# The output projection of a hybrid decoder block in 128x512 instead of 128x256 products, with a fourth weight buffer

## The chip, the core and the metric

The kernel runs on one core of one Trainium2 chip. The metric is the device time of one execution in microseconds (us). The core has five engines that run their own instruction queues in order and meet through semaphores: TensorE (PE, matrix products; PEld is its loading of the stationary operand), VectorE (DVE), ScalarE (ACT), GpSimd (POOL) and SyncE (SP), which here issues all DMA transfers.

## What is computed

A decoder block over 2048 tokens of width 1024: a state-space branch and an attention branch that picks 256 keys per query, both projected, gated and added (`merged`), then the output projection with the residual, then a gated feed-forward network. Everything is float32. The change touches the third of these lines:

```python
merged = (jax.nn.sigmoid(g_ssm) * (y_ssm @ w_proj_ssm[l])
          + jax.nn.sigmoid(g_att) * (y_att @ w_proj_attn[l]))
x = x + merged @ w_out[l]                      # 2048x1024 @ 1024x1024
h2 = _rms(x, norm2_g[l])
x = x + (jax.nn.silu(h2 @ w_ffn_gate[l]) * (h2 @ w_ffn_up[l])) @ w_ffn_down[l]
```

## The kernel before

**Products.** Each float32 operand is held as two parts, hi and lo, in a reduced format. `mm3` (line 406) makes one product out of three matmul instructions: hi by hi, hi by lo, lo by hi. A matmul has a stationary operand of 128 columns and a moving operand of up to 512 columns, and every matmul instruction comes with its own weight load.

**Stages.** The dense half of the network (`block`, line 1695) runs over four token blocks of 512 tokens, called first to fourth block here. In each block come, in this order: the two branch projections (rows `f<-act,ww` of the trace, 192 matmuls of 128x512), whose gated sum is split into `mg`; the output projection (`f<-ww,mg`, 384 matmuls of 128x256); the second norm and the transposes of the normed rows `ha`, `hb`, `hh` into `h` (`f<-ident,ha` and so on); gate and up products (`f<-h,ww`); down products (`f<-wd,at`), added into `x1`.

**The output projection** (lines 1800 to 1827) is cut into four column groups of 256. In each group it makes two passes, tokens 0 to 255 and 256 to 511. A pass is 48 matmuls into one PSUM bank that holds two token tiles side by side; then DVE adds the bank into `x1` (`x<-f,x`). The two weight buffers of a group serve both passes and are dropped in the second. After the first pass of the last group the norm of token tiles 0 and 1 begins: `factor` (a square with row sum on ACT, then `ss` on DVE and `rr` on POOL) and `norm` (`ha`, `hb` on DVE).

**Weights** come through a ring (`Rings`, line 290), in the fixed order of `weights()` (line 1662). In the first block a buffer is made on the chip: a raw tile of 512 KB is loaded (two raw buffers), ACT, POOL or DVE makes the hi part, POOL or DVE the lo part, and the pair of 1 MB (`ww`, for the down weights `wd`) is also stored to DRAM (`wc`). In the other three blocks the pair is loaded from `wc`. The ring for `ww` has three buffers (line 1984); a buffer is filled again after `drop`, and loads are issued in the order of the list only.

**Order.** Every instruction is recorded by `Pace` (line 52), which keeps a clock for each engine from fixed costs. Three streams of work (state space, attention with its top-k search, dense) are merged by it: a stream goes on when its inputs are due and, for search work, as long as DVE's queue is less than `AHEAD` = 7 us ahead of PE, or `TIGHT` = 0.5 us while `tight` is set. `tight` is set after the first pass of the last column group and cleared when the first gate and up products are recorded. While the search runs, four more PSUM banks are lent to the dense stream (`lend`, `bank`), beside its own three. Dense work on block n waits until attention has finished that block's tiles.

## Time and profile before

| | us |
|---|---|
| median of 3 runs | 3380.91 |
| lowest and highest | 3377.41, 3381.88 |
| the profiled execution, its own time | 3383.72 |
| span of the trace | 3381.7 |
| mean granted TensorE clock | 0.972 |
| output projection, first to fourth block: start to end | 1056.3 to 1106.8, 1668.9 to 1717.2, 2304.1 to 2352.7, 2965.2 to 3011.4 |

In rows of the trace a group reads: engine, operation, output tile<-input tiles, shapes, count. A bracket such as [6.13 <-DVE ss] gives the idle time of that engine just before the row, and what ended it. The granted clock is a share of 2.4 GHz; a stretch at 0.5 is the lower level, 1.2 GHz.

### The profile page before, as it was taken

How to read it: one execution, taken by the hardware profiler on the slowest of the kernel's cores; microseconds unless marked ns; L12 is line 12 of the kernel's file. 1: busy time of each engine (PE TensorE's matmuls, PEld its weight loads, DVE VectorE, ACT ScalarE, POOL GpSimd, SP SyncE). 2: the span in 40 equal slices, each digit the busy share in tenths (PEclk: the TensorE clock that was granted, in tenths of full speed). 3: DMA queues.
4: the chain of work that ended last, by engine and by line, in shares of the span. 5: the costliest groups of instructions: out<-in, count | busy, mean ns of one | idle time of the engine just before them, and what ended most of it. 6: DMA issues, size and time to landing. Idle time of an engine off the chain costs nothing. (4 is left out here: it accounts for less than half of the span.)

```text
span 3381.7 us, 44230 instructions
## 1 busy us (share of the span) xinstructions
PE 3185.2 (94%) x16296; PEld 2693.5 (80%) x16296; DVE 2122.2 (63%) x4540; ACT 1278.5 (38%) x2213; POOL 621.0 (18%) x620
## 2 busy tenths in 40 slices
PE   7999989899978999998989999998999999899999
PEld 6989768678757888876788888878788888698887
DVE  6565785555687666699686775867776666322223
ACT  3231445444552444355412443666124444010000
POOL 4333766522232221134100000000000000000000
PEclk9999999999989999999999999999999999999999
DMA  5734333535458766756745324375472332755554
GB/s 185 230 114 115 114 111 106 166 92 149 123 186 293 276 210 217 248 174 239 297 155 230 143 94 168 132 263 215 177 262 99 125 131 94 275 195 201 200 200 161
DMA packets 315015, 605.66 MB, mean 179 GB/s; under 512 B 46352, under 2 KB 198704, under 8 KB 284080
## 3 DMA queue, kind: packets, MB, share of 16 engines
q1 hardware_dynamic: 314800, 602.85, 51.2%
q8 instruction: 128, 2.10, 0.2%
q14 instruction: 87, 0.71, 0.1%
HBM read 434.70 MB, written 166.89 MB: 178 GB/s over the span
## 5 line engine op out<-in xcount | busy, mean ns | idle before, releaser
L206 PE MATMUL f<-h,ww 128*128 128x512 f32 (+1 forms) x4416 | 1016.7, 384 | 1.2 <-DVE h L206 0.8
L206 PEld LDWEIGHTS f<-h,ww 128*128 128x128 f32 x4416 | 802.4, 191 | 156.4 <-DVE h L206 1.8
L206 PE MATMUL f<-wd,at 128*128 128x512 f32 x2112 | 523.5, 400 | 41.1 <-DVE wd L206 10.6
L206 PEld LDWEIGHTS f<-wd,at 128*128 128x128 f32 x2112 | 399.6, 192 | 132.6 <-DVE x L206 12.7
L206 PE MATMUL gps<-hT,gw 128*128 128x512 f32 x1536 | 384.7, 401 | 4.6 <-ACT gsg L206 3.2
L206 ACT ACTIVATE jka<-S,tr 128x1536 bf16<-128x1536 f32 (+5 forms) x217 | 305.6, 1408 | 190.5 <-DVE tr L206 115.6
L206 PEld LDWEIGHTS gps<-hT,gw 128*128 128x128 f32 x1536 | 287.0, 192 | 68.0 <-ACT gsg L206 5.2
L206 DVE TENSOR_TENSOR x<-f,x 128x512 f32<-128x512 f32 x352 | 236.5, 687 | 103.2 <-PE f L206 102.5
L206 PE MATMUL mm<-w,hT 128*128 128x512 f32 (+1 forms) x1152 | 282.3, 402 | 8.9 <-DVE hT L206 6.4
L206 DVE TENSOR_TENSOR tl<-pt,th 128x512 fp32r<-128x512 f32 (+1 forms) x288 | 184.1, 658 | 137.2 <-ACT th L206 136.4
L206 PEld LDWEIGHTS mm<-w,hT 128*128 128x128 f32 x1152 | 240.3, 238 | 36.0 <-DVE hT L206 8.0
L206 DVE SCALAR_TENSOR_TENSOR t<-t,f 128x512 f32<-128x512 f32 (+1 forms) x125 | 83.5, 668 | 278.8 <-PE f L206 238.1
L206 ACT CAST th<-pt 128x512 fp32r<-128x512 f32 (+1 forms) x288 | 155.9, 564 | 234.7 <-PE pt L206 230.5
L206 PE MATMUL f<-act,ww 128*128 128x512 f32 x768 | 189.3, 406 | 29.2 <-POOL ww L206 9.7
L206 PEld LDWEIGHTS f<-act,ww 128*128 128x128 f32 x768 | 148.9, 196 | 69.4 <-POOL ww L206 22.2
L206 PE MATMUL f<-ww,mg 128*128 128x256 f32 x1536 | 188.9, 285 | 10.1 <-ACT ww L206 4.6
L206 PEld LDWEIGHTS f<-ww,mg 128*128 128x128 f32 x1536 | 187.1, 194 | 12.4 <-ACT ww L206 5.0
L206 ACT ACTIVATE P<-P,m 128x1024 f32<-128x1024 f32 (+7 forms) x192 | 172.3, 900 | 53.5 <-DVE m L206 53.4
L206 POOL TENSOR_TENSOR g<-g,g 128x512 f32<-128x512 f32 x31 | 39.9, 1286 | 811.8 <-DVE g L206 798.1
L206 PE MATMUL lg<-kk,q 128*128 128x512 f32 (+1 forms) x640 | 184.1, 389 | 2.4 <-DMA kk<-kk 2.4
L206 ACT ACTIVATE t<-f 128x512 f32<-128x512 f32 (+1 forms) x92 | 53.1, 577 | 333.6 <-PE f L206 333.5
L206 ACT CAST at<-t 128x512 fp32r<-128x512 f32 (+1 forms) x92 | 55.3, 601 | 326.4 <-DVE t L206 326.4
(361 smaller groups left out, 4508.9 us busy)
## 6 DMA issues: line engine op xcount, KB each, us to landing
ww<-wc SPq DMA_DIRECT2D x180, 1024.0 KB, 4.9
wd<-wc SPq DMA_DIRECT2D x66, 1024.0 KB, 8.4
wc<-ww SPq DMA_DIRECT2D x60, 1024.0 KB, 7.8
raw<-in_w_in_dram SPq DMA_DIRECT2D x104, 256.0 KB, 3.3
wc<-wd SPq DMA_DIRECT2D x22, 1024.0 KB, 7.4
x<-in_x_dram SPq DMA_DIRECT2D x32, 512.0 KB, 5.1
gate<-gsg SPq DMA_DIRECT2D x64, 256.0 KB, 2.2
g<-gate SPq DMA_DIRECT2D x64, 256.0 KB, 5.3
```

The costliest lines, as they stand in the source:

```text
L206: return f(*args, **kw)
```

## The change

The output projection is now cut into two column halves of 512. In each half a pass takes two token tiles into two PSUM banks, one bank per tile, and goes through four weight buffers `q` of 256 rows by 512 columns each; each buffer serves tile t and then tile t + 1 before the next is asked for. All four buffers of a half are held until the second pass, which drops them one after the other. A block has 192 matmuls of 128x512 where it had 384 of 128x256, in four passes of 48 instead of eight, and still eight additions into `x1`, of 512 columns of one tile instead of 256 columns of two. The first bank of a pass is taken from the dense stream's own three, the second from either pool. The norm of tiles 0 and 1 and `tight` come after the first pass of the second half, so that 48 matmuls of 128x512 follow instead of 48 of 128x256. The loader is asked after every product (`tick`) instead of after every pair. The ring for `ww` has four buffers in all stages.

```diff
-        for cg in range(4):
-            for b in range(2):
-                items.append(("w", lambda raw, cg=cg, b=b: [
-                    (raw.rearrange("p (k c) -> p k c", k=4),
-                     a["w_out"][0, b * 512:(b + 1) * 512, cg * 256:(cg + 1) * 256]
+        for half in range(2):
+            for q in range(4):
+                items.append(("w", lambda raw, half=half, q=q: [
+                    (raw.rearrange("p (k c) -> p k c", k=2),
+                     a["w_out"][0, q * 256:(q + 1) * 256, half * 512:(half + 1) * 512]
                      .rearrange("(k p) c -> p k c", p=128))]))
...
-                for cg in range(D // NC):
-                    cl = slice(cg * NC, (cg + 1) * NC)
+                for half in range(2):
+                    cl = slice(half * 512, (half + 1) * 512)
                     for t in range(0, nt, 2):
-                        for k in range(KD):
-                            if k % 2 == 0:
-
-                                late = t == nt - 2 and k >= 4
-                                w = ld.get("w", 0 if late or k < 4 else 1)
-                                w = w.rearrange("p z a (k c) -> p (z a) k c", k=4)
-                                yield ready(w, mg) if k == 0 else at("PE", w)
-                            if k == 0:
-                                ps = bank()
+
+                        ps = []
+                        for q in range(4):
+                            w = ld.get("w", q if t < nt - 2 else 0)
+                            w = w.rearrange("p z a (k c) -> p (z a) k c", k=2)
                             for j in range(2):
+                                yield ready(w, mg) if q == 0 else at("PE", w)
+                                if q == 0:
+                                    ps.append(bank(j == 1))
                                 tl = slice((t + j) * 128, (t + j + 1) * 128)
-                                self.mm3(ps[:, j * NC:(j + 1) * NC], mg[:, 0, k, tl], mg[:, 1, k, tl],
-                                         w[:, 0, k % 4], w[:, 1, k % 4], k == 0 and j == 0, k == KD - 1 and j == 1)
-                            if t == nt - 2 and k % 4 == 3:
+                                for k in range(2):
+                                    g = q * 2 + k
+                                    self.mm3(ps[j], mg[:, 0, g, tl], mg[:, 1, g, tl], w[:, 0, k], w[:, 1, k],
+                                             g == 0, g == KD - 1)
+                                    ld.tick()
+                                if q == 3:
+
+                                    nc.vector.scalar_tensor_tensor(x1[:, t + j, cl], ps[j], 0.5, x1[:, t + j, cl],
+                                                                   op0=ALU.mult, op1=ALU.add)
+                            if t == nt - 2:
                                 ld.drop("w")
-                            ld.tick()
-
-                        nc.vector.scalar_tensor_tensor(x1[:, t:t + 2, cl], ps.rearrange("p (t c) -> p t c", t=2),
-                                                       0.5, x1[:, t:t + 2, cl], op0=ALU.mult, op1=ALU.add)
-                        if cg == D // NC - 1 and t == 0:
+                        if half == 1 and t == 0:
                             self.pace.tight = True
...
-                wp = self.pool(st, "fw", 3)
+                wp = self.pool(st, "fw", 4)
...
-                ld.ring("w", wp, 3)
+                ld.ring("w", wp, 4)
```

The order of the instructions shifts in all later stages, since `Pace` merges the streams anew. Three places are shown.

DVE, second block, before: the end of a round of the search (`jkd`, `uf`, `tf`), the addition of the last column group for tiles 0 and 1 (`x<-f,x`), and the norm of these tiles.

```order
L206 SCALAR_TENSOR_TENSOR jkd,cnt_13631<-H_13800,tf_13632,jkd 128x640
L206 TENSOR_SCALAR uf_13633<-cnt_13631 128x2
L206 SCALAR_TENSOR_TENSOR tf_13632<-uf_13633,tf_13632 128x2
L206 SCALAR_TENSOR_TENSOR x_14698<-f,x_14698 128x2x256
L206 TENSOR_SCALAR ss_15507<-ss_15507 128x1
L206 SCALAR_TENSOR_TENSOR ha<-x_14698,rr_15508,gB 128x1024
L206 TENSOR_SCALAR ss_15514<-ss_15514 128x1
L206 SCALAR_TENSOR_TENSOR hb<-x_14698,rr_15515,gB 128x1024
L206 SCALAR_TENSOR_TENSOR x_14698<-f,x_14698 128x2x256
```

The same place on DVE now:

```order
L206 SCALAR_TENSOR_TENSOR jkd,cnt_13395<-H_13529,tf_13396,jkd 128x640
L206 TENSOR_SCALAR uf_13397<-cnt_13395 128x2
L206 SCALAR_TENSOR_TENSOR tf_13396<-uf_13397,tf_13396 128x2
L206 SCALAR_TENSOR_TENSOR x_14508<-f,x_14508 128x512 x2
L206 TENSOR_SCALAR ss_15083<-ss_15083 128x1
L206 SCALAR_TENSOR_TENSOR ha<-x_14508,rr_15084,gB 128x1024
L206 TENSOR_SCALAR ss_15090<-ss_15090 128x1
L206 SCALAR_TENSOR_TENSOR hb<-x_14508,rr_15091,gB 128x1024
L206 SCALAR_TENSOR_TENSOR x_14508<-f,x_14508 128x512 x2
```

The norm still stands right behind the additions, with search work in front of them; between the two groups of additions PE now has a pass of 48 wide products instead of 48 narrow ones.

ACT, first block, before: the last parts of `mg`, the hi parts of weight buffers (`ww<-raw`; the first of these rows is the first buffer of the output projection) and the last steps of the search (`fin`).

```order
L206 CAST ww<-raw 128x1024
L206 CAST mg<-g_9735 128x512
L206 CAST ww<-raw 128x1024 x2
L206 ACTIVATE fin,ssum<-S_7045,nT 128x1024
L206 CAST ww<-raw 128x1024 x3
L206 ACTIVATE fin,ssum<-S_7204,nT 128x896
```

The same place on ACT now:

```order
L206 CAST ww<-raw 128x1024
L206 CAST mg<-g_9735 128x512
L206 CAST ww<-raw 128x1024 x3
L206 ACTIVATE fin,ssum<-S_7045,nT 128x1024
L206 CAST ww<-raw 128x1024 x2
L206 ACTIVATE fin,ssum<-S_7204,nT 128x896
```

Four buffers of the output projection, all that the first pass needs, now stand ahead of the first `fin`; three did.

PE, end of the third block and start of the fourth, before: the last value products of attention (`po<-tl,v`), its two closing products (`lg<-ident,s` turns the row sums, `lg<-r,hsel` spreads their reciprocals), down products, and the first projection of the fourth block (`f<-act,ww`).

```order
L206 MATMUL po<-tl,v 128x256
L206 MATMUL f<-h_20700,ww 128x512 x12
L206 MATMUL lg<-ident,s 8x128
L206 MATMUL f<-wd,at 128x512 x18
L206 MATMUL lg<-r_25857,hsel 128x128 x8
L206 MATMUL f<-wd,at 128x512 x78
L206 MATMUL f<-act_25848,ww 128x512 x24
```

The same place on PE now:

```order
L206 MATMUL po<-tl,v 128x256
L206 MATMUL f<-wd,at 128x512 x24
L206 MATMUL lg<-ident,s 8x128
L206 MATMUL lg<-r_25427,hsel 128x128 x8
L206 MATMUL f<-act_24977,ww 128x512 x24
```

The close of the last attention tile moved behind the down products of the third block: 96 of them stood between the turned sums and the fourth block, and none does now.

## Rows read from the trace of the kernel before

**Rows 1.** Page, engines: busy us (share of the span), instructions.

```profile
PE 3185.2 (94%) x16296; PEld 2693.5 (80%) x16296; DVE 2122.2 (63%) x4540; ACT 1278.5 (38%) x2213; POOL 621.0 (18%) x620
```

**Rows 2.** Groups of PE by line: names, shapes, count | busy, mean ns | idle before.

```profile
L206 PE MATMUL f<-wd,at 128*128 128x512 f32 x2112 | 523.5, 400 | 41.1 <-DVE wd L206 10.6 <-DVE x L206 9.5 <-DMA wd<-wc 7.2
...
L206 PE MATMUL f<-ww,mg 128*128 128x256 f32 x1536 | 188.9, 285 | 10.1 <-ACT ww L206 4.6 <-DMA ww<-wc 2.6 <-POOL ww L206 2.0
```

**Rows 3.** Stretches of the four output projections: engines, PEclk, DMA share, GB/s.

```profile
1056.30:1106.80 50.50, 48.49 (x384) 48.22 (x385) 38.40 (x74) 15.23 (x20) 11.06 (x7) 0.93 0.85 302
1668.90:1717.20 48.30, 46.77 (x385) 46.17 (x383) 43.33 (x125) 8.92 (x12) 1.29 (x1) 1.00 0.55 192
...
2965.20:3011.40 46.20, 46.20 (x387) 46.18 (x386) 8.61 (x14) 2.92 (x5) 2.38 (x3) 1.00 0.53 186
```

**Rows 4.** Timeline, fourth block: start us, us, engine, group [idle before <-releaser].

```profile
2965.22 46.23 PE L206 MATMUL f<-ww,mg 128*128 128x256 f32 x384
...
3045.59 0.60 ACT L206 ACTIVATE t<-f 128x512 f32<-128x512 f32 x1 [4.09 <-PE f L206]
...
3056.47 0.60 ACT L206 ACTIVATE t<-f 128x512 f32<-128x512 f32 x1 [4.09 <-PE f L206]
```

**Rows 5.** Who PE waited for: us in total, times, longest us.

```profile
PE f L206 <- DVE ss L206: 13.2, 2, 7.1
...
PE f L206 <- DMA act<-att: 3.6, 3, 1.4
...
PE f L206 <- DMA ww<-wc: 2.6, 3, 1.3
```

**Rows 6.** Timeline, second block, after the output projection.

```profile
1719.11 0.69 DVE L206 SCALAR_TENSOR_TENSOR x<-f,x 128x512 f32<-128x512 f32 x1
...
1721.89 1.28 DVE L206 SCALAR_TENSOR_TENSOR ha<-x,rr,gB 128x1024 f32<-128x1024 f32 x1 [0.73 <-DMA ww<-wc]
...
1723.32 1.94 PE L206 MATMUL f<-ident,ha 128*128 128x128 f32 x8 [6.13 <-DVE ss L206]
...
1731.94 1.07 PE L206 MATMUL f<-ident,hh 128*128 128x128 f32 x8 [0.63 <-DVE hh L206]
```

**Rows 7.** Timeline, third block, the same place.

```profile
2359.82 1.94 PE L206 MATMUL f<-ident,ha 128*128 128x128 f32 x8 [7.10 <-DVE ss L206]
```

**Rows 8.** Timeline, fourth block, the same place.

```profile
3011.29 1.04 PE L206 MATMUL f<-ident,ha 128*128 128x128 f32 x8
...
3017.72 1.06 PE L206 MATMUL f<-ident,hh 128*128 128x128 f32 x8 [0.23 <-DVE hh L206]
```

**Rows 9.** Stretch behind the wait in the second block: engines, PEclk, DMA share.

```profile
1722.00:1729.00 7.00, 5.53 (x22) 4.50 (x23) 5.71 (x8) 3.32 (x7) 0.55 (x1) 0.51 0.01 2
```

**Rows 10.** First block, start of the output projection: timeline, last a DMA group (median to landing).

```profile
1056.36 2.35 POOL L206 TENSOR_TENSOR ww<-raw,ww 128x1024 fp32r<-128x1024 f32 x1 [1.67 <-DMA g<-gate]
...
1058.77 1.44 PE L206 MATMUL f<-ww,mg 128*128 128x256 f32 x5 [1.97 <-POOL ww L206]
...
1063.38 0.38 SPq L206 DMA_DIRECT2D raw<-in_w_out_dram  x1
...
1104.22 1.03 ACT L206 CAST ww<-raw 128x1024 fp32r<-128x1024 f32 x1
...
raw<-in_w_out_dram SPq DMA_DIRECT2D x2, 512.0 KB, 5.8
```

**Rows 11.** End of the third block: timeline, last two DMA groups (median to landing).

```profile
2881.39 0.27 PE L206 MATMUL lg<-ident,s 128*8 128x128 f32 x1
...
2891.09 0.38 SPq L206 DMA_DIRECT2D att<-ya  x1
...
2899.15 1.62 PE L206 MATMUL f<-wd,at 128*128 128x512 f32 x3 [5.34 <-DMA wd<-wc]
...
act<-att SPq DMA_DIRECT2D x4, 512.0 KB, 8.3
...
att<-ya SPq DMA_DIRECT2D x1, 256.0 KB, 2.3
```

More of the change, by code (lines that the diff above doesn't have):

```diff
@@ L1701, in block @@
         hf, h0 = t0 // HALF, t0 % HALF
-        NC = 256
         spare = self.pace.spare
```

## Prediction

> **What bounds the kernel now.** I read the page's engine line first: PE is busy in 94% of the span and DVE in 63% [rows 1], and 3381.7 − 3185.2 = 196.5 us of PE idle time is left. So time goes in two ways only: PE's work takes less, or PE waits less. Next come the PE groups by line: the 1536 narrow matmuls of the change wait little themselves, 10.1 us [rows 2]. Then the stretches: in the fourth block the output projection holds PE for 46.20 of 46.20 us and its weight loads fill 46.18, at a granted clock of 1.00 (2.4 GHz), with DVE at 8.61 [rows 3]. In the second block PE is as full, but DVE is at 43.33 of 48.30, which is the top-k search of the next block. The timeline gives the price of one matmul: 384 narrow ones take 46.23 us, 120.4 ns each; for the wide form, two neighbouring pairs of a gate and an up product end in ACT steps 3056.47 − 3045.59 = 10.88 us apart, 48 matmuls, 226.7 ns each [rows 4]. Last come the waits: 13.2 us in two pieces of PE for `ss`, DVE's step of the second norm [rows 5]. The timeline puts them right behind the output projection of the second and third block, 6.13 and 7.10 us [rows 6, 7]; in the fourth block, where there is no search, PE goes into `ha` with no wait [rows 8].
>
> **Pace.** Removed in each block are 384 matmuls of 120.4 ns, 46.23 us; added are 192 of 226.7, 43.52. Columns are the same; what goes is the fixed part of half the instructions, (2 × 120.4 − 226.7) = 14 ns for each pair. That is 2.7 us on the path, since nothing else is late in the stretch. In the first block the mean clock is 0.93 [rows 3], and I take 2.1 there: 3 × 2.7 + 2.1 = **−10.2**, bounds 0 (the wide price does not carry over from gate and up products to this place) and −10.8. The eight additions become sixteen halves by tile with the same columns in all; DVE has room for them in every block but by the wait below.
>
> The Trainium skill speaks against this term. The rows show a fixed part of some 14 ns per matmul. In "TensorE: Matmul & The Clock Gate", section "Back-to-back issue gap", the isolated gap of a warm matmul is N/2.4 + 2.5 ns. An estimate from this page is 109 and 216 ns, 41.9 against 41.4 us a block, a gain of 2.0 us in all four; the sum would be 8 us higher. Both rows lie above the page's numbers, by 11 ns each, and the measurement decides.
>
> **The wait for the norm.** PE's last narrow pass (48 × 120.4 ns = 5.78 us) is the cover under which DVE must add the column group, and ACT, DVE and POOL make the row sums and `ha`. From the end of the pass before to the start of `ha`'s transposes it takes 5.78 + 6.13 = 11.9 us in the second block and 5.78 + 7.10 = 12.9 in the third [rows 6, 7]. The chain stands behind what the search left in DVE's queue: The pass that it adds ended at 1723.32 − 11.9 = 1711.4, but `x<-f,x` starts only at 1719.11, with the last pass already over. The new cover is 48 × 226.7 = 10.88 us. DVE's order at this place is the same as before: search, additions, norm. So 1.0 and 2.0 us of wait remain, a gain of 5.1 in each: **−10.2**. Bounds: 0, when the search is let further ahead of PE by the same amount (its lead is set in microseconds, and a longer pass may hold more of it), and −13.2, when all of the wait goes [rows 5]. I take the middle since the queue in front of the addition is set by the search's 7 us lead, and that has not changed. Late next is `hb`, one norm step of 1.28 us later [rows 6], which has 8 transposes in front of it.
>
> **The clock behind that wait.** Behind the 6.13 us of idle time the granted clock is 0.51 (1.2 GHz) over 7 us [rows 9], and the transposes up to `hh` take 1731.94 − 1723.32 = 8.62 us, against 3017.72 − 3011.29 = 6.43 in the fourth block without a wait [rows 6, 8]: 2.2 us for the drop. With 1 to 2 us of wait the drop may still come. For two blocks I take 1.5 each, **−3**, bounds 0 and −4.4.
>
> **Weights in blocks two to four.** Each tile has been loaded whole and a fourth buffer is there, so its load is issued one drop earlier. The 2.6 us of waits for `ww<-wc` [rows 5] go: **−2.5**, bounds 0 and −2.6. All four buffers are held through a first pass, so nothing is loaded for 10.88 us; then four drops come 2.72 us apart, and the first buffer of the next half is wanted 8.16 us after its drop. DMA is busy 0.53 to 0.55 of these stretches [rows 3], so I cost the bunching at nothing.
>
> **Weights in the first block.** Here a buffer is raw load 5.8 us, a cast on ACT 1.03, a lo part on POOL 2.35, together 9.2, and there are two raw buffers, so one comes every 4.6 us [rows 10]. A first pass now asks for four within 3 × 2.72 us; before, four narrow passes went by on four buffers. The first starts PE at 1058.77 as before. The fourth's raw load is issued, if as in the row, at 1063.38, and the buffer is ready at 1072.6; it is wanted at 1066.9 at full clock, about 1068.6 with some microseconds at the lower level behind the start. PE waits 4: **+4**, bounds 0 (ACT casts all four ahead of the first `fin` now) and +9 (7.5 from 4 × 4.6 − 10.9, and a clock drop). The second half gets its buffers in time, its raw tiles are loaded while the first half is held.
>
> **End of the third block.** The last attention tile now closes right before the fourth block's projections. Before, 96 down products (21.8 us by 226.7 ns) covered the way from `lg<-ident,s` at 2881.39 to the store of `att` at 2891.09, its landing of 2.3 and the load of 8.3 [rows 11], and 3.6 us of waits for that load were left [rows 5]. Now 24 products of the other branch stand behind the closing products, 5.4 us. Against it stands the wait of 5.34 us for `wd` at 2899.15 [rows 11], where down products ran bare at the pace of their loads: attention's rows now stand among them and give the loads time. I take **+2**, bounds −6 and +10 (9.7 + 2.3 + 8.3 − 1.1 for the eight `lg<-r` − 5.4 = 13.8 of wait, 3.6 before).
>
> **Everything behind.** The merged order changes in all feed-forward stages and in attention, and with it who waits for which addition and weight. The same kinds and numbers of instructions run there, so I take 0, bounds ±8, a fifth of the 41.1 us that down products wait in the trace [rows 2].
>
> **Sum.** −10.2 − 10.2 − 3 − 2.5 + 4 + 2 = −19.9 against the profiled execution's own 3383.7, 3363.8. The median of the runs lies 2.8 below that execution, so 3361 is to be expected. Its own range, from the bounds not all on one side, is 3352 to 3372.
>
> **Rivals.** First, *only the pace counts*. The wait for the norm is set by DVE, busy 43 of 48 us there; if the merge lets the search run as far ahead as the cover has grown, the 6 and 7 us stay, the clock drop with them, and the first block's +4 eats what the loads give. 3383.7 − 10.2 + 4 − 2.8 = 3375. For it: DVE's share in [rows 3]. Against it: the fixed lead.
>
> Second, *slower: the end of attention runs bare*. The 96 down products that stood behind the third block's last attention tile have been used up ahead of it; if that tile's chain (value products, store, load) then runs with no dense work beside it, PE idles for most of these 21.8 us too, beside the 13.8 − 3.6 = 10.2 of the load, of which 2 are in the sum: 3361 + 21.8 + 8.2 = 3391. For it: the order, with nothing but 24 projections behind the closing products. Against it: as the order shows, down products stand between the last value products and the close. It makes the kernel slower once PE waits over some 27 us more at this place than before.
>
> Third, *a wide matmul costs what two narrow ones do* here. 3361 + 10.2 = 3371; PE's busy time and the four stretches would be as before but for waits. For it: the wide price is taken from gate and up products, none of which read `mg`; if columns alone are the limit, half as many weight loads bring nothing. Against it: PEld is as full as PE in the narrow stretch [rows 3], and the two prices differ by 14 ns a pair at the same clock [rows 4].
>
> By the page named above the third case would be 3369.
>
> Fourth, *the down products wait less as well*. With `ww` one buffer deeper, loads for them start earlier; if a third of the 41.1 us goes [rows 2], 13 us, the time is 3348. For it: the wait of 5.34 [rows 11]; against it: a busy queue at that place, and `wd` has a ring of its own.
>
> **How the numbers follow.** Forecast 0.55, only the pace 0.21, slower 0.14, wide for nothing 0.04, down products 0.06. A difference of 0.2%, 6.8 us, is about what a measurement of this kernel can tell from no change; so the bound for faster is 3374. Faster: 0.55 + 0.04 + 0.06 + 0.06 of the second case = 0.71. Same: 0.15 of it and 0.02 of the slower case, which may come at half its price, 0.17. Slower: 0.12. The range leaves out the slower case and a little at the lower end: 3343 (the fourth rival and 5 below) to 3383 (the first with 8 us from the stages behind).
>
> **What the profile after would show.** Output projections of 43.5 us in the fourth block and about 10.9 us from one pass to the next; rows `f<-ww,mg` 768 times. The idle time before `f<-ident,ha` at 0 to 3 us in the second and third block: over 5 speaks for the first rival. A granted clock of 1.00 behind it. In the first block a wait of 2 to 6 us for POOL or ACT `ww` within the first pass. At the start of the fourth block, waits for `att` of 4 to 8 us: over 20 means the second rival. My prediction is wrong if the busy time of these rows does not fall by 8 us, or if waits in gate, up and down products change by over 8 us, which I have no row to foresee.

## The result, and the profile after

The changed kernel takes 3358.1 us (median of 6 runs, 3351.9 to 3364.5) beside 3381.4 for the kernel before: a ratio of 0.9935, 95% interval 0.9924 to 0.9945, by which it is some 22 us faster (the two medians alone differ by 23). The forecast was 3361. The profiled execution took 3357.9, against 3383.7 before, 25.8 less; its span is 3355.8. The engine line and the rows of the changed products and of the down products read so (they answer to [rows 1, 2]):

```profile
PE 3171.5 (95%) x15528; PEld 2651.1 (79%) x15528; DVE 2106.4 (63%) x4532; ACT 1275.1 (38%) x2211; POOL 638.1 (19%) x628
...
L206 PE MATMUL f<-ww,mg 128*128 128x512 f32 x768 | 180.3, 397 | 10.6 <-ACT ww L206 7.0
...
L206 PE MATMUL f<-wd,at 128*128 128x512 f32 x2112 | 518.2, 397 | 28.7 <-DVE t L206 6.5 <-ACT t L206 6.0 <-DVE jkd L206 5.4
```

PE is busy 13.7 us less, and 3355.8 − 3171.5 = 184.3 us of idle time are left, 12.2 less. The changed rows, the same products in half as many instructions, are busy 8.6 us less, as foreseen. The down products wait 28.7 us instead of 41.1, which was not foreseen. The four output projections by stretch (engines PE, PEld, DVE, ACT, POOL, then the granted clock, DMA share, GB/s) answer to [rows 3]:

```profile
1056.30:1111.44 55.14, 49.12 (x192) 39.24 (x193) 40.92 (x72) 16.31 (x22) 20.32 (x10) 0.89 0.73 262
1665.45:1709.13 43.68, 43.68 (x193) 35.85 (x191) 37.48 (x107) 17.11 (x23) 1.84 (x2) 1.00 0.53 198
2290.85:2334.53 43.68, 43.68 (x193) 35.85 (x191) 37.33 (x97) 37.72 (x39) 1.83 (x2) 1.00 0.53 193
2942.06:2985.58 43.52, 43.52 (x194) 35.98 (x192) 8.91 (x13) 2.92 (x5) 2.39 (x3) 1.00 0.52 192
```

The last three are 43.5 us long as forecast, and PEld no longer fills them (36 of 43.5). The first is longer than before, 55.1 against 50.5, at a clock of 0.89. Behind the stretch of the second and third block the timeline shows, against [rows 6, 7]:

```profile
1708.54 1.28 DVE L206 SCALAR_TENSOR_TENSOR ha<-x,rr,gB 128x1024 f32<-128x1024 f32 x1 [0.73 <-POOL rr L206]
...
1709.88 1.09 PE L206 MATMUL f<-ident,ha 128*128 128x128 f32 x8 [0.75 <-DVE ss L206]
...
1712.50 0.66 PE L206 MATMUL f<-ident,hb 128*128 128x128 f32 x4 [1.52 <-DVE x L206]
...
1718.73 1.06 PE L206 MATMUL f<-ident,hh 128*128 128x128 f32 x8 [0.83 <-DVE hh L206]
```

```profile
2335.54 1.09 PE L206 MATMUL f<-ident,ha 128*128 128x128 f32 x8 [1.01 <-DVE ss L206]
...
2345.22 1.03 PE L206 MATMUL f<-ident,hh 128*128 128x128 f32 x8
```

The waits of 6.13 and 7.10 us are down to 0.75 and 1.01. The norm itself is hardly faster: from the end of the pass that it needs (1709.13 − 10.9 = 1698.2) to the start of the transposes are 11.6 us in the second block, where 11.9 stood before, and 11.9 in the third for 12.9. It is PE that has other work by then.

**Where the time went, by blocks.** To tell this change from what the merge of the three streams does later, I cut each trace at the first branch projection (`f<-act,ww`) of each block. The four stretches are the four blocks with all that runs beside them. Before, then after:

```profile
981.04:1625.27 644.23, 589.03 (x2917) 490.22 (x2917) 488.61 (x925) 281.42 (x413) 177.86 (x86) 0.95 0.70 244
1625.27:2259.80 634.53, 615.52 (x3268) 526.32 (x3269) 453.15 (x1021) 285.84 (x450) 15.21 (x16) 0.99 0.48 177
2259.80:2915.28 655.48, 633.67 (x3461) 541.11 (x3460) 440.02 (x912) 239.19 (x395) 13.50 (x12) 0.98 0.46 166
2915.28:3381.67 466.39, 456.63 (x2240) 386.10 (x2240) 122.72 (x182) 42.13 (x71) 13.45 (x12) 1.00 0.54 203
```

```profile
980.81:1621.93 641.12, 585.20 (x2724) 478.97 (x2725) 469.49 (x914) 284.14 (x418) 192.93 (x93) 0.95 0.69 245
1621.93:2247.33 625.40, 610.38 (x3077) 514.02 (x3076) 447.80 (x1002) 276.00 (x440) 15.38 (x16) 0.99 0.49 181
2247.33:2888.71 641.38, 629.00 (x3270) 531.56 (x3268) 446.07 (x931) 242.98 (x398) 13.46 (x12) 0.99 0.47 171
2888.71:3355.79 467.08, 456.74 (x2049) 378.02 (x2048) 123.83 (x184) 42.70 (x72) 13.44 (x12) 0.99 0.54 200
```

The second column is the length. The gain is 3.1 us in the first block, 9.1 in the second, 14.1 in the third, and the fourth is 0.7 longer, although its output projection is 2.55 shorter. So the pace, which should show in all four alike, shows in none by itself. That is what the experiments had to settle.

Within the blocks, the stretch from the first product of the output projection to `ha` goes from 50.5 to 55.1 us, from 54.4 to 44.4, from 55.7 to 44.7 and from 46.1 to 43.5, which is 18.9 us less in all. From `ha` to the end the first block is 8.0 us shorter, the second 1.0 longer, the third 2.3 and the fourth 0.2 shorter. Ahead of the output projection the fourth block is 3.4 us longer and the third 0.8 shorter.

### The profile page after: what moved, and what is told of

It is laid out like the page before. It is cut to its first block, busy times and chain, and to the rows that moved or that the text cites. A ratio compares the mean times of both kernels' runs of the same rounds, so it can differ in the third digit from the quotient of the medians.

```text
span 3355.8 us, 42712 instructions
## 1 busy us (share of the span) xinstructions
PE 3171.5 (95%) x15528; PEld 2651.1 (79%) x15528; DVE 2106.4 (63%) x4532; ACT 1275.1 (38%) x2211; POOL 638.1 (19%) x628
## 5 line engine op out<-in xcount | busy, mean ns | idle before, releaser
L206 PE MATMUL f<-wd,at 128*128 128x512 f32 x2112 | 518.2, 397 | 28.7 <-DVE t L206 6.5
L206 ACT ACTIVATE jka<-S,tr 128x1920 bf16<-128x1920 f32 (+6 forms) x217 | 305.6, 1408 | 180.5 <-DVE tr L206 128.7
L206 PE MATMUL f<-ww,mg 128*128 128x512 f32 x768 | 180.3, 397 | 10.6 <-ACT ww L206 7.0
L206 ACT ACTIVATE t<-f 128x512 f32<-128x512 f32 (+1 forms) x92 | 52.9, 575 | 343.8 <-PE f L206 343.7
L206 PEld LDWEIGHTS f<-ww,mg 128*128 128x128 f32 x768 | 147.2, 192 | 43.2 <-ACT ww L206 7.9
```

The source lines that it names most:

```text
L206: return f(*args, **kw)
```

## The experiments

The same cut of every profile gives this table. "Start" is the time up to the first block, in which PE's work stands in the same order in all of them: it moves between 973 and 981 us from one execution to the next, so lengths of blocks compare better than spans. Each length is that of one execution; a block of the changed kernel came out within 2 us in its two profiles. Each ratio is to runs of the kernel before taken beside it.

| profile | start | first | second | third | fourth | ratio to before, interval |
|---|---|---|---|---|---|---|
| before | 981.0 | 644.2 | 634.5 | 655.5 | 466.4 | 1 |
| after | 980.8 | 641.1 | 625.4 | 641.4 | 467.1 | 0.9935, 0.9924 to 0.9945 |
| e5_after | 979.3 | 643.1 | 624.7 | 639.4 | 467.0 | 0.9937, 0.9923 to 0.9950 |
| e1_narrow | 975.7 | 641.4 | 624.9 | 640.1 | 468.7 | 0.9939, 0.9927 to 0.9952 |
| e2_ring4 | 973.0 | 643.6 | 638.3 | 652.5 | 469.2 | 1.0008, 0.9997 to 1.0020 |
| e3_cover | 973.8 | 649.3 | 627.8 | 645.6 | 469.4 | 0.9981, 0.9972 to 0.9990 |
| e4_four | 981.0 | 642.7 | 627.9 | 639.9 | 466.7 | 0.9943, 0.9926 to 0.9959 |
| e6_tight | 977.3 | 644.6 | 623.7 | 651.4 | 468.4 | 0.9971, 0.9959 to 0.9982 |
| e7_tight_narrow | 974.4 | 644.4 | 627.7 | 651.2 | 468.7 | 0.9974, 0.9963 to 0.9984 |
| e8_before_tight | 979.1 | 645.8 | 628.4 | 653.1 | 466.2 | 0.9977, 0.9968 to 0.9986 |
| e9_late | 980.0 | 656.9 | 631.2 | 643.7 | 470.9 | 1.0004, 0.9995 to 1.0014 |
| e10_raw3 | 980.7 | 640.0 | 630.6 | 656.9 | 466.2 | 0.9980, 0.9971 to 0.9989 |
| e11_lead3 | 980.4 | 641.8 | 624.5 | 639.3 | 464.8 | 0.9922, 0.9908 to 0.9935 |
| e12_lead3_dve | 981.0 | 641.7 | 627.6 | 638.3 | 464.6 | 0.9932, 0.9919 to 0.9946 |

**e1_narrow: the pace undone, all else in the same order.** Each wide product is made as two narrow ones; the record that sets the order sees one wide product, so DVE's and ACT's rows are those of the changed kernel.

```diff
-                                    self.mm3(ps[j], mg[:, 0, g, tl], mg[:, 1, g, tl], w[:, 0, k], w[:, 1, k],
+                                    self.mm3n(ps[j], mg[:, 0, g, tl], mg[:, 1, g, tl], w[:, 0, k], w[:, 1, k],
...
+        mm = self.tc.nc.tensor.matmul
+        for a, b in ((ah, bh), (ah, bl), (al, bh)):
+            self.pace.note("PE", "matmul", (ps, a, b), {})
+        for h in range(2):
+            c = slice(h * 256, (h + 1) * 256)
+            mm(ps[:, c], ah, bh[:, c], start=start and h == 0, stop=False)
+            mm(ps[:, c], ah, bl[:, c], start=False, stop=False)
+            mm(ps[:, c], al, bh[:, c], start=False, stop=stop and h == 1)
```

> The changed kernel with each 128x512 product of the output projection made as two of 128x256, everything else in the same order: the pace alone is undone. Theory (pace): the output projection of the fourth block takes 46.1 us again instead of 43.5, the waits before ha stay at 0 to 1 us since the cover grows to 11.5 us, and the time is 3358 + 10 = 3368. Rival (the width is worth nothing, all comes from order and buffers): 3358, the stretch 43.5.

Measured: 3358.5, 0.9939. My theory said 10 us slower; it is not slower at all within some 5 us, which is what the intervals of the two ratios leave open. Its blocks:

```profile
975.75:1617.18 641.43, 584.82 (x2917) 488.56 (x2917) 469.52 (x913) 283.81 (x418) 191.78 (x93) 0.95 0.69 244
1617.18:2242.06 624.88, 612.84 (x3270) 524.39 (x3268) 448.11 (x1002) 276.51 (x440) 15.41 (x16) 0.99 0.50 182
2242.06:2882.18 640.12, 627.59 (x3462) 537.34 (x3460) 445.81 (x931) 243.10 (x398) 13.47 (x12) 0.99 0.47 171
2882.18:3350.91 468.73, 458.71 (x2241) 387.56 (x2240) 124.12 (x184) 42.84 (x72) 13.50 (x12) 0.99 0.54 200
```

From its first product to `ha` the fourth projection takes 46.07 us again, as before the change, and 43.52 in the changed kernel: the price of the narrow form is real, 2.55 us. But the first three blocks are as long as with wide products (641.4, 624.9, 640.1), and of the 2.55 in the fourth 1.7 are left. The second and third block from the first product of the output projection to the first down product, the changed kernel and then e1:

```profile
1665.45:1776.88 111.43, 105.27 (x514) 88.48 (x512) 91.54 (x233) 30.89 (x48) 4.46 (x5) 0.98 0.53 198
2290.85:2407.92 117.07, 108.63 (x513) 92.13 (x512) 95.62 (x235) 68.12 (x80) 4.46 (x5) 0.94 0.50 185
```

```profile
1660.70:1771.64 110.94, 107.40 (x706) 98.61 (x704) 91.86 (x233) 30.81 (x48) 4.47 (x5) 0.98 0.55 204
2285.58:2401.07 115.49, 107.53 (x705) 98.75 (x704) 94.41 (x233) 68.00 (x80) 4.46 (x5) 0.97 0.51 188
```

With narrow products PE reaches `ha` 46.1 us after the first product in both blocks and does not wait there, with wide ones after 44.4 and 44.7, with waits; by the first down product the narrow form is no later. What the wide form saves, PE waits in the steps that follow (in the third block it runs at a lower granted clock as well, 0.94 for 0.97). So of the 10 us that PE saves, the whole shows some 1 us, which is not clear of noise.

**e2_ring4: the fourth weight buffer alone.**

```diff
-                wp = self.pool(st, "fw", 3)
+                wp = self.pool(st, "fw", 4)
...
-                ld.ring("w", wp, 3)
+                ld.ring("w", wp, 4)
```

> The kernel before with four weight buffers instead of three and nothing else. Theory (pace and cover): only the 2.6 us of waits for ww<-wc go, and the merge shifts by up to 8 us either way: 3379 (3371 to 3387), waits before ha of 5 to 8 us in the second and third block stay. Rival (the fourth buffer is the gain): 3365 or less with those waits gone.

Measured: 3380.2, 1.0008: no gain in the whole. Yet much of what the merge does in the changed kernel is here already. The waits for `ww<-wc` are gone from the output projections, the down products wait 30.1 us instead of 41.1, the first block behind `ha` takes 511.6 us instead of 518.5 (the changed kernel 510.5 and 511.6), and the last attention tile closes behind the down products, with a start of the fourth block of 52.9 us as in the changed kernel. It is lost again, most of it at the norm: PE waits 23.1 us before `ha` instead of 13.2 [rows 5], in the first, second and third block:

```profile
1104.95 1.94 PE L206 MATMUL f<-ident,ha 128*128 128x128 f32 x8 [5.51 <-DVE ss L206]
...
1713.81 1.94 PE L206 MATMUL f<-ident,ha 128*128 128x128 f32 x8 [7.47 <-DVE ss L206]
...
2354.79 1.94 PE L206 MATMUL f<-ident,ha 128*128 128x128 f32 x8 [10.13 <-DVE ss L206]
```

Against no wait in the first block and 6.13 and 7.10 in the others before [rows 6, 7], that is 5.5, 1.3 and 3.0 us more. PE got there earlier and waited for DVE. e1 and e2 both have narrow products and four buffers; between their ratios, 0.9939 and 1.0008, lie some 23 us, as much as the whole gain. That is the new order of the output projection, its longer cover with all that goes with it.

**e3_cover: the cover without the new order.** Narrow products, four buffers, and the last two column groups interleaved, so that 96 narrow products follow the norm's start.

```diff
+                for cg, t in [(0, 0), (0, 2), (1, 0), (1, 2), (2, 0), (3, 0), (2, 2), (3, 2)]:
...
-                        if cg == D // NC - 1 and t == 0:
+                    if (cg, t) == (3, 0):
```

> The kernel before with four weight buffers, narrow products, and the last two column groups taken tokens 0 to 255 of both first, then tokens 256 to 511 of both, so that 96 narrow products (11.5 us) cover the norm instead of 48: the cover alone. Theory (cover): waits before ha in the second and third block fall from 6.1 and 7.1 to 0 to 1.5 us, and the clock behind stays at 1.00: 3381 - 2.5 - 11 - 3 = 3365 (3357 to 3373). Rival (the search runs as far ahead as the cover grows): the waits stay at 4 to 7 us, 3378.

Measured: 3373.4, 0.9981; that is some 6 us of gain, and the forecast of 3365 was missed, just beyond its edge. The second block gains 6.7 us and the third 9.9, with no wait left before `ha` in the second and 3.86 in the third:

```profile
2344.51 1.09 PE L206 MATMUL f<-ident,ha 128*128 128x128 f32 x8 [3.86 <-DVE ss L206]
```

Cover and buffer bring 16.6 us in these two blocks without any wide product, and the first block gives 5.1 of it back, the fourth 3.0. The fourth block's loss is at its start, 53.1 us long, as in e2. In the first block another order of the merge, with 7.3 us of wait before `hb`, is what I see; why it came out so is left open. So the cover is worth its price where the search runs, but how much of the whole 22 us it carries by itself no run tells: in this order of the products it is a third.

**e9_late: wide products and four buffers without the cover.** The four lines that begin the norm of tiles 0 and 1 stand behind the last pass.

```diff
                         if half == 1 and t == 0:
                             self.pace.tight = True
-                            factor(0)
-                            norm(0, fn.tile([128, D], F32, name="ha"))
-                            factor(1)
-                            norm(1, fn.tile([128, D], F32, name="hb"))
+                factor(0)
+                norm(0, fn.tile([128, D], F32, name="ha"))
+                factor(1)
+                norm(1, fn.tile([128, D], F32, name="hb"))
```

> The changed kernel with the norm of tiles 0 and 1 recorded after the last pass instead of before it: wide products and four buffers, but no cover. Theory (the cover is the gain): the idle time before ha in the second and third block is 5 to 12 us (the search lag of some 8 us is now held off by no tight stretch), in the fourth some 4, and the time is 3378 (3370 to 3388), so that all of the gain is gone. Rival (the new merge of later stages is the gain): 3365 or less.

Measured: 3380.5, 1.0004. With the whole change but without cover nothing of the gain is left. The waits in the second and third block:

```profile
1728.14 1.97 PE L206 MATMUL f<-ident,ha 128*128 128x128 f32 x8 [4.13 <-DVE ha L206]
...
2361.17 1.97 PE L206 MATMUL f<-ident,ha 128*128 128x128 f32 x8 [5.93 <-DVE ha L206]
```

They are below those of before, which fits `tight` beginning 10.9 us ahead of the norm, so that DVE's queue is short by then; the first block, where `ha` had no wait, now has one of 5.3 and is 14 to 16 us longer than in the changed kernel. Without the cover of its own pass each block pays. This run has even less cover than the kernel before, which has a pass of 48 narrow products there; so it shows that the cover is needed, and not what the added part of it is worth.

**e6_tight and e7_tight_narrow: DVE's queue held short.** `tight` is set at the start of the second half, one pass earlier; e7 is the same with narrow products in the same order.

```diff
+                        if half == 0 and t == nt - 2:
+                            self.pace.tight = True
                         if half == 1 and t == 0:
-                            self.pace.tight = True
```

> The changed kernel with the search held back (tight) from the start of the second half, one pass earlier. Theory (DVE's queue sets when the second norm is done): in the second and third block the waits before ha and hb (0.8 to 1.5 us each) go, those before hh shrink, DVE reaches the addition within 3 us of the pass: 3352 (3347 to 3357). Rival (the search comes due later and PE waits there instead): 3358, the waits move into gate and up products or attention.

> The same as the run before, in the same order, with each 128x512 product of the output projection made as two of 128x256. The first run of narrow products gave 3358.5, as fast as wide ones. Theory (in the second and third block DVE, not PE, ends last, so that a slower pace is hidden there): with DVE ahead of PE the pace is worth its price in all blocks, and this run is 8 to 10 us slower than the one before. Rival (the width is worth nothing to the whole): equal within 3 us.

Measured: 3367.0 and 3369.0, 0.9971 and 0.9974, beside 3355.6 for the changed kernel, run again next to them (e5_after):

> The changed kernel once more, beside the next three. Every theory expects 0.9935 of the kernel before, as measured first, and a stretch of some 981 us ahead of the fourth stage mark that moves by several us from one execution to the next although nothing was changed in it.

The waits before `ha` went as forecast, and the second block is 1.0 us shorter than in e5_after; but the third is 12.0 us longer, and the whole slower than both the forecast and its rival. Holding back the search delays attention: its first value product comes 307.2 us into the third block, where it came at 292.6. Its last one stands 4.4 us ahead of the end with no dense product behind it, where the changed kernel has 24 such products and 8.9 us. The last two stretches of 20 us ahead of the end of the third block, e5_after and then e6_tight:

```profile
2846.40:2866.40 20.00, 18.88 (x120) 16.36 (x120) 15.59 (x33) 9.91 (x18) 0.00 (x0) 1.00 0.14 46
2866.40:2886.40 20.00, 17.88 (x102) 14.76 (x100) 11.67 (x20) 3.48 (x7) 0.00 (x0) 1.00 0.94 373
```

```profile
2856.94:2876.94 20.00, 19.58 (x123) 16.81 (x121) 15.01 (x31) 8.20 (x15) 0.00 (x0) 1.00 0.44 158
2876.94:2896.94 20.00, 14.69 (x78) 11.97 (x77) 9.63 (x21) 7.71 (x14) 0.00 (x0) 0.82 0.00 0
```

In the last one PE makes 78 instructions instead of 102, the granted clock is 0.82, and DMA moves nothing. This is the slower rival of the prediction, the end of attention running bare. The changed kernel escapes it by 24 products.

The pair e6 and e7 also tests the pace where DVE is ahead. There the second block does pay for narrow products, 627.7 against 623.7, more than the 2.7 us of the stretch itself. The first and third do not (644.4 against 644.6, 651.2 against 651.4), and the whole differs by 2.0 us of medians, within the interval. My forecast of 8 to 10 was wrong: with DVE ahead at the norm, the pace shows in one block of three, and what takes it up in the other two is open.

**e8_before_tight: the kernel before, with `tight` set one column group earlier.**

```diff
+                        if cg == D // NC - 2 and t == nt - 2:
+                            self.pace.tight = True
                         if cg == D // NC - 1 and t == 0:
-                            self.pace.tight = True
```

> The kernel before with the search held back from the start of the last column group, 48 narrow products earlier, and nothing else. Theory (DVE's queue): the waits of 6.1 and 7.1 us before ha fall to 1 to 3 us, 3371 (3365 to 3377), so two thirds of their gain are to be had without wide products. Rival (only a longer cover helps): they stay at 5 to 7 us, 3380.

Measured: 3369.7, 0.9977, as forecast. The waits fall to 1.33 and 4.66 us, the second by less than forecast, and the blocks by 6.1 and 2.4. So either shortens the wait: a longer cover, or a shorter queue in front of DVE's part.

**e4_four and e10_raw3: the weights of the first block.** One uses each buffer of the first half for four token tiles in the first block, the other gives three raw buffers.

```diff
+                    wide = nt if tb == 0 and half == 0 else 2
-                    for t in range(0, nt, 2):
+                    for t in range(0, nt, wide):
...
-                ld = Rings(self, self.pool(first, "fraw", 2), 1, self.weights())
+                ld = Rings(self, self.pool(first, "fraw", 3), 1, self.weights())
...
-                ld.bufs = 2
+                ld.bufs = 3
```

> The changed kernel, but in the first block the first half of the output projection uses each weight buffer for all four token tiles before the next, so that a buffer is wanted every 5.4 us instead of every 2.7. Theory (making of weights sets the first pass): the waits of 2.46 and 1.93 us in that pass and the low clock behind them go, the stretch from its first product to ha falls from 55.2 to 49 us: 3352. Rival (the buffers only come late elsewhere): the waits move into the second half or into gate and up products, 3358.

> The changed kernel with three raw buffers instead of two, which only the first block uses. Theory (loads of raw weights set the first block): the waits of 2.5 and 1.9 us in the first pass go, and the whole first block, from its first projection to that of the second block, which took 641 to 645 us in every variant so far, falls by 5 to 15 us: 3348. Rival (the engines that make the parts set it, or attention): 640 to 645 us again, 3357.

Measured: 3358.1 and 0.9943 for the first, 3371.9 and 0.9980 for the second, slower than its forecast and its rival. In e4 the two waits of the first pass are gone, one of 3.17 comes in the second half and one of 7.14 before `hh`, and the first block is 642.7 us long as ever; the forecast of 3352 was missed. In e10 the projections of the first block are 20 us shorter (55.6 against 75.4 us from the first to the output projection), and the block is 640.0 us long all the same; PE, 20 us earlier, waits 11.85 us for DVE before `hb`; attention's first value product comes later in all three blocks, and in the third the bare end appears again, 656.9 us. The first block stayed within 640 to 646 us in ten of twelve variants. What sets its length is open: it is not the waits for weights at its beginning, which these two variants moved without moving its end.

**e11_lead3: the start of the fourth block.** Its first products take three column tiles of the state-space branch instead of two, ahead of those that wait for the last attention tile.

```diff
+                    lead = 3 if tb == NB - 1 else 2
-                    for q, (ct, br) in enumerate([(0, 0), (1, 0), (0, 1), (1, 1)] +
+                    for q, (ct, br) in enumerate([(ct, br) for br in range(2) for ct in range(lead)] +
...
-                    gp = self.pool(sp, "mgate", 2)
+                    gp = self.pool(sp, "mgate", 3)
```

The gates get a third buffer with it, in all blocks; what that does by itself no run tells.

> The changed kernel, but the fourth block begins with three column tiles of the state-space branch instead of two, before the first of attention (12 more products, 2.7 us, ahead of the load that follows the last attention tile). Theory (that load is what the projections of the fourth block wait for, 4.4 us, and the low clock of 0.92 comes from it): the stretch of 53.4 us falls to 49, 3353. Rival (waits elsewhere replace it, or the order of attention shifts): 3357.

Measured: 3352.1, 0.9922, the best of all. The stretch from the first product of the fourth block to its output projection, before, after and in e11:

```profile
2915.28:2965.22 49.94, 46.30 (x193) 36.74 (x194) 14.87 (x22) 4.35 (x7) 9.01 (x7) 0.97 0.90 322
```

```profile
2888.71:2942.06 53.35, 48.91 (x194) 38.83 (x194) 16.10 (x24) 4.97 (x8) 8.98 (x7) 0.92 0.84 303
```

```profile
2885.89:2936.90 51.01, 47.56 (x193) 37.90 (x193) 15.78 (x24) 4.97 (x8) 9.02 (x7) 0.93 0.86 314
```

2.3 us of the 4.4 forecast came, which is what its profile has to show for a median 3.5 to 6 us lower; the intervals of e5_after and e11_lead3 overlap, so that it is not shown to be faster than the changed kernel. The low clock did not go with the load, 0.93 for 0.92: it begins ahead of it. The first 24 products of the block, before and after:

```profile
2915.28 5.76 PE L206 MATMUL f<-act,ww 128*128 128x512 f32 x24 [0.78 <-DVE x L206]
```

```profile
2888.71 8.25 PE L206 MATMUL f<-act,ww 128*128 128x512 f32 x24
...
2888.71:2892.00 3.29, 3.29 (x9) 2.61 (x9) 1.38 (x2) 0.62 (x1) 0.00 (x0) 0.50 0.28 81
```

In the changed kernel the granted clock is 0.50 over their first 3.3 us, right behind a wait of 1.78 us of the closing products for DVE.

**e12_lead3_dve: what still waits behind the projection.** In the third block of the changed kernel PE waits again, for the second tile of `hh`, since ACT runs a search step ahead of its casts:

```profile
2346.72 2.00 ACT L206 ACTIVATE jka<-S,tr 128x2048 bf16<-128x2048 f32 x1 [3.40 <-DVE tr L206]
...
2352.08 1.97 PE L206 MATMUL f<-ident,hh 128*128 128x128 f32 x8 [5.83 <-DVE h L206]
```

In e12, which has e11's edit too, DVE makes these casts in the first three blocks:

```diff
-            nc.scalar.copy(hi[b], pv)
+            if own:
+                nc.vector.tensor_copy(hi[b], pv)
+            else:
+                nc.scalar.copy(hi[b], pv)
```

> The kernel of the run with three leading column tiles, and in the first three blocks DVE instead of ACT makes the hi part of the turned rows of token tiles 2 and 3, since ACT runs a search step of 4.1 us between the two tiles there. Theory (what is left of the waits behind the projection is that step on ACT): the wait of PE before the second tile's transposes falls from 5.5 to 2 us in the third block and from 4.3 to 2 in the first, 0.9922 - 0.0015 of the kernel before, 3347. Rival (DVE, the busier engine, is later with everything behind): 3352 to 3360.

Measured: 3355.1, 0.9932. The place is as read:

```profile
2350.80 0.63 PE L206 MATMUL f<-ident,hh 128*128 128x128 f32 x4 [2.51 <-DVE h L206]
```

The wait is 2.5 us instead of 5.8 (5.5 in e11), and the third block 1.0 shorter than in e11; the second is 3.1 longer. Nothing is won: the time is in the range of the rival. That DVE, the busier engine, is the reason fits, but no run tests it apart.

## Why the prediction was right, step by step

The time, 3358.1 against 3361, and the sign came out; of the steps, one carried it, several were wrong, and that the sum came so near is in part luck. By its own signs it was half right: the changed rows are busy 8.6 us less where 8 was asked, but the waits of the down products changed by 12.4 us, where a change of over 8 in gate, up and down products was to mean that it is wrong.

**Right: the wait for the norm.** Forecast −10.2; the waits fell from 13.2 to 1.8 us, 11.5 less, with residues of 0.75 and 1.01 where 1.0 and 2.0 were worked out. Not all of it is won: the waits of the next steps, before `hb` and `hh`, rise from 12.8 to 18.8 us over the four blocks. e9 shows that the cover is needed: without any the ratio is 1.0004. The first rival (only the pace counts, the search runs ahead as the cover grows) has fallen, by its own sign: waits of over 5 us before `ha` were to speak for it.

**Wrong in what it is worth: the pace, −10.2.** The stretch is as forecast: 46.07 to 43.52 us, 2.55 in the fourth block. By the formula for the isolated gap in the Trainium skill, "TensorE: Matmul & The Clock Gate", section "Back-to-back issue gap", an estimate is 0.5 us there; the trace does not agree with it. The third rival, a wide matmul at the price of two narrow ones, has fallen with this stretch. The step that failed is "that is 2.7 us on the path, since nothing else is late in the stretch". Something was late: DVE, by the wait that the next step of the same sum counts. In the second block PE came to `ha` after 54.4 us before, after 46.1 in the new order with narrow products (e1) and after 44.4 with wide ones; order and buffer alone give 8.3 of the 10.0, and behind `ha` the other 1.7 are gone again. e1 measures the whole: 10 us more of PE work, 0.0002 to 0.0004 in the ratio, about 1 us, with some 5 us of doubt. The prediction's remark that eight additions become sixteen halves is a slip without effect on the sum; they stay eight.

**Wrong: the clock, −3.** The drop is gone. The granted clock behind the second projection, against [rows 9]:

```profile
1710.00:1716.00 6.00, 3.74 (x26) 2.88 (x27) 4.97 (x7) 3.27 (x6) 0.52 (x1) 1.00 0.56 214
```

It is 1.00 where it was 0.51, but the way from `ha` to `hh` takes 1718.73 − 1709.88 = 8.85 us, against 8.62 before [rows 6]. PE is at full speed and waits for DVE in 1.52 and 0.54 us pieces before the two halves of `hb` and 0.83 before `hh`. I had named `hb` as late next and then given it no price.

**Wrong in what they are worth: the weights in blocks two to four, −2.5.** The loads are in time; e2 shows that this alone is worth nothing, for the same reason as the pace: PE waits for the norm instead.

**Right in size: the first block, +4.** The fourth buffer came as worked out:

```profile
1063.33 0.38 SPq L206 DMA_DIRECT2D raw<-in_w_out_dram  x1
...
1071.05 1.04 ACT L206 CAST ww<-raw 128x1024 fp32r<-128x1024 f32 x1 [6.93 <-DMA raw<-in_w_out_dram]
1072.14 0.50 PE L206 MATMUL f<-ww,mg 128*128 128x512 f32 x1 [2.46 <-ACT ww L206]
1072.17 2.35 POOL L206 TENSOR_TENSOR ww<-raw,ww 128x1024 fp32r<-128x1024 f32 x1 [12.28 <-ACT ww L206]
...
1074.57 5.75 PE L206 MATMUL f<-ww,mg 128*128 128x512 f32 x17 [1.93 <-POOL ww L206]
```

The raw load is issued at 1063.33, and PE waits 2.46 + 1.93 = 4.4 us; the buffer is ready at 1074.5 where I had 1072.6. The stretch to `ha` is 4.7 us longer, where the sum has 4 − 2.1 of pace. The block as a whole is not longer for it, 641 to 643 us against 644: from `ha` on it is 7 to 8 us shorter, with 30 to 31 us of PE idle time instead of 33 and a clock of 0.97 instead of 0.96. e2 has the same 511.6 us there, so this goes with the fourth buffer and not with the wide products. I had it at 0 ± 8 among everything behind; for the rest, the first block's length hardly moves with what is done in it early.

**About right: the end of the third block, +2.** The start of the fourth block is 3.4 us longer, and the waits for `wd` at the end of the third, 5.34 us [rows 11] and one of 1.02, are gone. But the load was not the reason: waits for `att` are 4.4 us where 3.6 stood [rows 5]; 2.5 of the 3.4 are the first 24 products at the lower clock, 8.25 us for 5.76, which the sum did not have. e2 shows the same start, so this too goes with the fourth buffer. The slower rival, at 0.14, did not come true in this kernel but did in e6 and e10, at a price of 10 to 17 us in the third block; I had put it at 30. It was nearer than the chance says: 24 products lay between. The fourth rival (the down products wait less as well), at 0.06, came true in its condition: they wait 12.4 us less, near the third of 41.1 that it names, and e2 shows that the buffer does it. Its time, 3348, did not come, since PE's idle time fell by only 12.2 us in all.

**Together.** In the trace the four stretches to `ha` are 18.9 us shorter, and −10.2 − 10.2 − 2.5 + 4, the terms that bear on them, are −18.9 as well. That is luck as to the parts: e1 gives the whole with no pace in it, and e2 gives nothing with the loads in time, so pace and loads bring next to nothing beside the cover, and the cover more than its 10.2. The places behind, which I had at −3 for the clock and +2, came to −8.0 in the first block, −2.3 in the third and +3.4 at the start of the fourth, most of it the fourth buffer's, and 25.8 us in the profiled executions stand against 19.9 forecast. What the record does not settle is why e3, with as long a cover and four buffers, has a first block 8 us longer than e1.

## What to carry to other kernels

When an engine arrives somewhere and waits for another, what the first saves ahead of that place is paid back there: count the wait and the savings in front of it once, not twice. A buffer that brings the engine there earlier is worth nothing until the wait has cover, as e2 shows. Undoing one part with the order of all other instructions kept tells what that part is worth, where a reading of busy time does not. And before holding work back on one stream, look at how many products of the others are left behind its end: the third block here was 10 to 17 us longer when none was.

## What the runs showed of the hardware

The fixed part of a matmul: with the same columns and a granted clock of 1.00, 192 wide products take 43.52 us and 384 narrow ones 46.07, 2.55 us or 13.3 ns for each of the 192 instructions saved (226.7 and 120.0 ns each). The time of an unchanged first part, 973 to 981 us from one execution to the next, moves by more than several of the effects in question; I had not expected it, and only the cut by blocks made the others visible.
